# Gate vectors as weighted row sums inside the feed-forward networks, one condition's sums on ScalarE and GpSimd, and a shared tile for two score maps

## The chip, the core and the metric

The kernel runs on one core of a Trainium2 chip. The metric is the device time of one execution in microseconds (us), as the median of several runs. One execution is also recorded by the hardware profiler: its span goes from its first to its last instruction, and all times in the trace count from the start of that span.

Five engines work side by side, each with its own queue, in which instructions run in order: TensorE (PE, with its weight loads shown apart as PEld), VectorE (DVE), ScalarE (ACT), GpSimd (POOL) and SyncE (SP), which here only issues transfers (SPq).

## The reference

Two layers of a trunk act on three blocks of 128 tokens: block 0 is context under one condition vector, blocks 1 and 2 are latent tokens under another. In each layer a vector of six parts (shift, scale and gate, twice) is made from each condition by one large product, and modulates a mixer and a SwiGLU network:

```python
for l in range(DEPTH):
    mod = jax.nn.silu(cond) @ w_mod[l] + b_mod[l]
    sh1, sc1, g1, sh2, sc2, g2 = jnp.split(mod[:, None, :], 6, axis=-1)
    u = layer_norm(x) * (1.0 + sc1) + sh1
    ...   # layer 0: h = mixer_ab(u ...), layer 1: h = mixer_cd(u ...)
    x = layer_norm(ALPHA * x + g1 * h, ln_g[l, 0], ln_b[l, 0])
    u = layer_norm(x) * (1.0 + sc2) + sh2
    x = layer_norm(ALPHA * x + g2 * swiglu(u, w_gate[l], w_up[l], w_down[l]), ln_g[l, 1], ln_b[l, 1])
```

The model is 1024 wide, so each part needs a 1024x1024 slice of w_mod (4 MB) for two vectors. The part with index 5 is the gate g2, which is needed only when the network of its layer ends. Layer 1's mixer holds differential attention: for each of six heads two score maps of 64-wide queries and keys, softmax on each, and p0 - lam * p1:

```python
s = jnp.einsum('bqhmd,bkhmd->bhmqk', qb, keys).astype(f32) * (HEAD_DIM ** -0.5)
p = jax.nn.softmax(s, axis=-1)
p = p[:, :, 0] - lam_full * p[:, :, 1]
```

## The kernel before

**Order of the work.** Layer 0's mixer (to about 204 us), its output projection with the two normalisations (`w_out_phase`, to about 271 us), its network (`ffn_phase`, to about 541 us), then the same for layer 1: mixer with the scores (to about 674 us), output projection (to about 747 us), network (to the end). The program is written in order, and a scheduler that runs before the kernel does gives each engine its fixed sequence: of the instructions that it expects to be ready, the earliest in the program goes first, and those in `boost` (so also `hmm`) go ahead of others. Semaphores and buffer reuse are set by it too. `gated()` places an instruction behind one that is named.

**Weights.** Each weight unit of 128x1024 comes by a transfer on SP's queue into one of five `raw` buffers, ScalarE casts it (L173) to a part `r`, VectorE subtracts (L175) to get a rest `l`, and TensorE multiplies with both; five pairs `wr`/`wl` hold them. A network runs in half steps: 48 products for `wg` or `wu`, then, as long as there are any, 18 for `dn` with one unit of w_down.

**Two ways to make a part of the modulation.** (1) `mod_pe`: eight raw units of w_mod (`rawm`), each multiplied on TensorE with the two condition columns as weights, 32 products of 256 columns on four column groups. `mod_now` uses it in the output stage for (0, 5) and (1, 5), where `WMODS` names them; its products have the tile name `mw` and line L229. In `WORDER` this is the letter M, between the network's head for block 1 (H1) and that for block 2 (H2). (2) `mod_steps`: eight steps, one for each unit (`mraw`, L243). For each condition c a tile `z[c]` gathers the unit's rows, weighted by a column of `cs`: ScalarE writes the first (L246), VectorE adds the other seven (L249). Then eight products with a column of ones (L254) sum over the partitions, and VectorE adds the bias. `SMODS` names the five parts of layer 1 that are made so during layer 0's network, at most four steps to a call and a pause after each part; calls come twice for each of ten pairs of chunks, and a part is summed up in the third call after the one before. Tiles `z`, `mraw` and those of the residuals (`so`, `sd`) share four buffers (`big`, tag `s`).

A gate (v of 2 or 5) is then written by eight small transfers (L285) on SP's queue to memory and read back as a broadcast (`load_g`, L417).

**Head of the network.** `head(b)` makes the first 256 columns of the gate and up products (`hg`, `hu`) for one block, as soon as `to_u(b)` has made that block's input `u2` (its last instruction is `ulf` on L333).

**Scores in layer 1.** `sc1(b, h)` makes both maps of one block and head, `sc2` the softmax's rest. Each map has a bank of its own out of four, a product on half of the rows (64 of 128), a maximum on VectorE (L1217) and an exponential on ScalarE (L1223). Layer 0's windowed attention (`win1`) already takes two maps in a tile of two banks (`ws`, with one maximum over both, L872).

Of the kernel before, what the change touches and what calls it, by code (L numbers as in the profile page):

```python
# [14 lines left out]
AF = mybir.ActivationFunctionType  # L15
ALU = mybir.AluOpType
AX = mybir.AxisListType
PSUM = bass.MemoryType.PSUM

P = 128  # L20
# [5 lines left out]
NFP = D_FF // 256  # L26
HOLD = 4
RHOLD = (3, 5)
WMODS = (((0, 5),), ((1, 5),))
TMODS = ()  # L30
SMODS = (((1, 1), (1, 0), (1, 3), (1, 4), (1, 2)), ())
NLNW = 8
AORDER = "Q0 R0 W4 T G0 D V0 M0 Q1 W12 M1 G1 C0 E M2 N1 R1 N2 V1 C1 X N0 N4 N3 N5"
NIDLE = (5, 4)
# [30 lines left out]
def trunk_kernel(ctx: ExitStack, tc: tile.TileContext, a: dict):  # L65
    nc = tc.nc
    mm = nc.tensor.matmul
    V, S, G, SY = nc.vector, nc.scalar, nc.gpsimd, nc.sync
# [4 lines left out]
    def opened(name, **kw):  # L73
        st = ExitStack()
        return st.enter_context(pool(name, **kw)), st
# [6 lines left out]
    def bankA(name):  # L82
        return psA.tile([P, 512], F32, tag="A", name=name)
# [19 lines left out]
    def small(shape, name):  # L103
        tick[0] += 1
        n = 1
        for s in shape[1:]:
            n *= s
        return perm.tile(shape, F32, tag=f"sm{n}", name=f"{name}{tick[0]}", bufs=SMALL[n])

    def big(shape, name):  # L110
        return perm.tile(shape, F32, tag="s", name=name, bufs=4)

    def mid(shape, name):
        return perm.tile(shape, F32, tag="uf", name=name, bufs=3)

    def boost(f, *args, **kw):
        with tc.high_priority(offset=BOOST):
            return f(*args, **kw)  # L118

    def hmm(*args, **kw):  # L120
        return boost(mm, *args, **kw)
# [24 lines left out]
    cs = const.tile([P, 2, KC], F32, name="cs")  # L146
# [22 lines left out]
    def gated():  # L169
        return tc.issue_after(gate[0].ins) if gate[0] is not None else nullcontext()  # L170
# [43 lines left out]
    def mod_tile(l, v):  # L214

        bm = perm.tile([P, 256], F32, tag="bm", name=f"bm{l}_{v}", bufs=2)
        if v in (2, 5):
            bsrc = a["b_mod"][l, v * D : (v + 1) * D].rearrange("(j n) -> j n", j=4)
            for j in range(4):
                S.dma_start(bm[32 * j : 32 * j + 32, :], bsrc[j : j + 1, :].broadcast_to([32, 256]))  # L220
        return bm
# [15 lines left out]
    def mod_steps(l, v, out):  # L237
        w = a["w_mod"][l].rearrange("(p k) n -> p k n", k=KC)
        bm = mod_tile(l, v)
        z = [big([P, D], f"z{l}_{v}_{c}") for c in range(2)]  # L240
        for k in range(KC):
            t = big([P, D], f"mraw{l}_{v}_{k}")
            SY.dma_start(t, w[:, k, v * D : (v + 1) * D])  # L243
            for c in range(2):
                if k == 0:
                    S.mul(z[c], t, cs[:, c, k : k + 1])  # L246
                else:
                    with gated():
                        V.scalar_tensor_tensor(z[c], t, cs[:, c, k : k + 1], z[c], ALU.mult, ALU.add)  # L249
            yield k == KC - 1  # L250
        ps = bankA(f"mod{l}_{v}")
        for c in range(2):
            for j in range(4):
                mm(ps[32 * j : 32 * j + 32, c * 256 : (c + 1) * 256], ones, z[c][:, j * 256 : (j + 1) * 256],  # L254
                   start=True, stop=True)

        if v in (2, 5):
            V.scalar_tensor_tensor(bm, ps[:, 0:256], selc[:, 0:1], bm, ALU.mult, ALU.add)
        else:
            V.tensor_scalar(bm, ps[:, 0:256], selc[:, 0:1], None, ALU.mult)  # L260
        V.scalar_tensor_tensor(bm, ps[:, 256:512], selc[:, 1:2], bm, ALU.mult, ALU.add)
        out.append((bm, ps))
# [887 lines left out]
    def mixer_cd(u, cat, pto, u1, t1):  # L1150
        o_k = a["o_diff_k"][0, 0].rearrange("t h m d -> t (h m d)")
        o_v = a["o_diff_v"][0, 0].rearrange("t h d -> t (h d)")
        slab = cd_slab
        bk = Banks("pcd", S=4)
        ap, ap_es = opened("attn_cd")
        rope_of[0] = ap.tile([P, 2, 2, 64], F32, name="rope1")
        S.dma_start(rope_of[0], a["k_rope"].rearrange("b p s d -> p b s d"))
        if True:
            nlam, sub = lamd["nlam"], lamd["sub"]
            dqT = ap.tile([P, H_DIFF, NTOK], F32, name="dqT")  # L1160
            dkT = ap.tile([P, H_DIFF, 512], F32, name="dkT")
# [4 lines left out]
            for i, n in ((0, 4), (4, 2)):  # L1166
                t = mid([P, 512], f"ck{i}")
# [38 lines left out]
            def sc1(b, h):  # L1206
                nk = 1 if b == 0 else 3
                k0 = 0 if b == 0 else P
                w = nk * P
                nm = small([P, 2], "dnm")  # L1210
                sums = small([P, 2], "dsum")
                pss = []
                for m in range(2):
                    rows = slice(64 * m, 64 * m + 64)
                    ps = bk("S", f"ds{b}_{h}_{m}")
                    hmm(ps[:, 0:w], dqT[rows, h, b * P : (b + 1) * P], dkT[rows, h, k0 : k0 + w], start=True, stop=True)
                    V.reduce_max(nm[:, m : m + 1], ps[:, 0:w], AX.X)  # L1217
                    pss.append(ps)
                V.tensor_scalar(nm, nm, -0.125, None, ALU.mult)
                pm = []  # L1220
                for m in range(2):
                    t = ap.tile([P, 384], F32, tag="p", name=f"dp{b}_{h}_{m}", bufs=5)
                    S.activation(t[:, 0:w], pss[m][:, 0:w], AF.Exp, bias=nm[:, m : m + 1], scale=0.125,  # L1223
                                 accum_out=sums[:, m : m + 1])
                    pm.append(t)
                st_of[b, h] = (pm, sums)
# [18 lines left out]
            def scores(upto):  # L1245
                while state["n2"] < upto:
                    while state["n1"] < min(state["n2"] + 2, len(items)) and (state["n1"] < upto or upto == len(items)):
                        sc1(*items[state["n1"]])
                        state["n1"] += 1
                    sc2(*items[state["n2"]])  # L1250
                    state["n2"] += 1
# [59 lines left out]
            for b in range(NB):  # L1311
                ps = bankA(f"cd4_{b}")
# [6 lines left out]
            for b in range(NB):  # L1319
                ps = bankA(f"cd3_{b}")  # L1320
# [23 lines left out]
    m = {}  # L1344
    xscr = dram.tile([NB, P, D], F32, tag="xscr", name="xscr")
    for l in range(2):
# [9 lines left out]
        if l == 0:  # L1356
            def mod_ab(v, bk):
                mp = mod_pe(0, v, bk("M", f"mod0_{v}"))
                if v == 2:
                    m[0, v] = mod_scratch(mp, f"0_{v}")  # L1360
                else:
                    m[0, v] = mod_cols(mp, 0, v, bk("M", f"modt0_{v}"))

            pre, wxr_es = mixer_ab(u, cat, early, early_es, ap1, ap1_es, pto, *first, [lambda bk, v=v: mod_ab(v, bk) for v in (2, 3, 4)])
        else:
            cat, cat_es = open_cat(1)
            mixer_cd(u, cat, pto, m["s1"], m["t1"])
            pre, wxr_es = [], None
# [11 lines left out]
        hh = tuple(lnp.tile([P, NHEAD, NTOK], F32R, name=f"hh{q}{l}") for q in "rl")  # L1380
        w_out_phase(l, pre, cat, x, gt, lnv, u2, m[l, 3], m[l, 4], wx, hh, bankTO, WMODS[l])
        if wxr_es is not None:
# [37 lines left out]
        def all_mods(todo):  # L1420
            for ll, v in todo:
                out = []
                for pause in mod_steps(ll, v, out):
                    yield pause
                nm = f"{ll}_{v}"
                if v in (2, 5):
                    m[ll, v] = mod_scratch(out[0][0], nm)
                else:
                    m[ll, v] = mod_cols(out[0][0], ll, v, out[0][1])

        gen = all_mods(SMODS[l])

# [90 lines left out]
```

## Time and profile before

| | us |
|---|---|
| three runs: median (lowest to highest) | 1020.04 (1017.32 to 1021.83) |
| profiled execution: its own time | 1018.55 |
| profiled execution: span | 1016.8 |
| TensorE busy | 996.9 |
| VectorE busy | 637.9 |
| ScalarE busy | 432.9 |
| GpSimd busy | 1.2 |

The span is 1.75 us shorter than the time of the same execution; that difference lies outside of the instructions. The profiled execution lies 1.49 us under the median of the three runs. Busy time of TensorE is modelled at the ends of its instructions, so a stretch that is all busy can still hold short gaps. The granted clock was 0.997 of full over the span.

### The profile page before, as it was taken

Reading aid. Unit: us, or ns where it says so; the run is one execution under the profiler, and the core shown is the slowest. Engines: PE = TensorE matmul, PEld = TensorE weight load, DVE = VectorE, ACT = ScalarE, POOL = GpSimd, SP = SyncE. Lnnn points to the kernel's source line nnn. Section 1 sums busy time; section 2 is a strip of 40 time slices with the busy share of each in tenths; the row PEclk is TensorE's granted clock in tenths of the full one; section 3 lists DMA queues with packets and bytes.
Section 4 is the critical chain, followed back from the end, with each engine's and each line's share of the span. In section 5 each row is a group of like instructions: output and inputs, shape, how many; then the busy total and the mean of one; then the engine's idle time right before and its main releaser. Section 6 shows DMA issues by size and latency. Waiting matters only on the chain.

```text
span 1016.8 us, 14891 instructions
## 1 busy us (share of the span) xinstructions
PE 996.9 (98%) x5679; PEld 829.7 (82%) x5679; DVE 637.9 (63%) x1356; ACT 432.9 (43%) x786; POOL 1.2 (0%) x5
## 2 busy tenths in 40 slices
PE   9999999999999999999999999999999999999996
PEld 4775567688898988989987766787889999999985
DVE  5477558588785977968567677558843333335554
ACT  3385533227543333333428555544833333333410
POOL 0000000000000000000000000000000000000000
PEclk9999999999999999999999999999999999999998
DMA  9975446472896767676615322235574444444401
GB/s 305 294 203 187 146 132 205 171 254 94 281 301 219 217 211 253 208 235 208 207 63 161 95 88 93 83 103 224 184 252 146 125 125 124 125 125 127 161 22 41
DMA packets 109703, 172.85 MB, mean 170 GB/s; under 512 B 10176, under 2 KB 78272, under 8 KB 109632
## 3 DMA queue, kind: packets, MB, share of 16 engines
q1 hardware_dynamic: 106960, 170.87, 52.8%
q10 hardware_dynamic: 2672, 1.04, 0.4%
q8 instruction: 44, 0.72, 0.3%
q14 instruction: 27, 0.22, 0.1%
HBM read 167.52 MB, written 4.36 MB: 169 GB/s over the span
## 4 chain that ended last, share of the span: by engine, by line
PE 91%; DMA 3%; DVE 3%; ACT 2%; issue 1%; ACTq 0%; DVEq 0%
PE dn L518 17%; PE wu L542 17%; PE wg L542 17%; PE cd L377 8%; PE wo L377 6%; PE rvg L377 3%; PE s L377 3%; PE rqk L377 2%; DMA rawm<-in_w_mod 2%; PE ds L118 2%; PE hg L377 2%; PE mod L118 1%; PE hu L377 1%; PE ms L118 1%; PE po L118 1%; PE wpo L118 1%
## 5 line engine op out<-in xcount | busy, mean ns | idle before, releaser
L542 PE MATMUL wg<-ulf,r_wg 128*128 128x384 f32 x320 | 108.4, 339 | 0.0
L542 PE MATMUL wu<-ulf,r_wu 128*128 128x384 f32 x320 | 108.3, 338 | 0.0
L542 PE MATMUL wu<-urf,r_wu 128*128 128x384 f32 x320 | 108.2, 339 | 0.0
L542 PE MATMUL wg<-urf,l_wg 128*128 128x384 f32 x320 | 108.1, 338 | 0.0
L542 PE MATMUL wu<-urf,l_wu 128*128 128x384 f32 x320 | 108.1, 338 | 0.0
L542 PE MATMUL wg<-urf,r_wg 128*128 128x384 f32 x320 | 108.0, 339 | 0.0
L175 DVE TENSOR_TENSOR l_wg<-raw_wg,r_wg 128x1024 fp32r<-128x1024 f32 x40 | 48.7, 1223 | 68.4 <-ACT r_wg L173 68.4
L249 DVE SCALAR_TENSOR_TENSOR z<-mraw,cs,z 128x1024 f32<-128x1024 f32 x70 | 86.3, 1280 | 8.3 <-DMA mraw<-in_w_mod 8.0
L175 DVE TENSOR_TENSOR l_wd<-raw_wd,r_wd 128x1024 fp32r<-128x1024 f32 x36 | 44.0, 1223 | 53.7 <-ACT r_wd L173 53.7
L173 ACT CAST r_wd<-raw_wd 128x1024 fp32r<-128x1024 f32 x36 | 37.8, 1050 | 87.0 <-PE wu L542 40.1
L175 DVE TENSOR_TENSOR l_wu<-raw_wu,r_wu 128x1024 fp32r<-128x1024 f32 x40 | 48.6, 1222 | 40.1 <-ACT r_wu L173 40.1
L173 ACT CAST r_wg<-raw_wg 128x1024 fp32r<-128x1024 f32 x40 | 42.0, 1050 | 73.0 <-PE dn L518 29.9
L173 ACT CAST r_wu<-raw_wu 128x1024 fp32r<-128x1024 f32 x40 | 42.0, 1049 | 64.6 <-issue 24.2
L518 PE MATMUL dn<-l_wd,hr 128*128 128x512 f32 x168 | 66.6, 396 | 0.0
L518 PE MATMUL dn<-r_wd,hr 128*128 128x512 f32 x168 | 66.5, 396 | 0.0
L518 PE MATMUL dn<-r_wd,hl 128*128 128x512 f32 x168 | 66.5, 396 | 0.0
L542 PEld LDWEIGHTS wg<-urf,r_wg 128*128 128x128 f32 x320 | 60.1, 188 | 1.9 <-issue 0.8
L542 PEld LDWEIGHTS wu<-urf,r_wu 128*128 128x128 f32 x320 | 60.1, 188 | 1.7 <-ACT r_wg L173 0.8
L542 PEld LDWEIGHTS wu<-ulf,r_wu 128*128 128x128 f32 x320 | 60.1, 188 | 0.5
L542 PEld LDWEIGHTS wg<-ulf,r_wg 128*128 128x128 f32 x320 | 60.1, 188 | 0.5
L542 PEld LDWEIGHTS wg<-urf,l_wg 128*128 128x128 f32 x320 | 60.1, 188 | 0.0
L542 PEld LDWEIGHTS wu<-urf,l_wu 128*128 128x128 f32 x320 | 60.1, 188 | 0.0
(418 smaller groups left out, 2180.0 us busy)
## 6 DMA issues: line engine op xcount, KB each, us to landing
raw_wd<-in_w_down SPq DMA_DIRECT2D x44, 512.0 KB
rawm<-in_w_mod SPq DMA_DIRECT2D x40, 512.0 KB
mraw<-in_w_mod SPq DMA_DIRECT2D x40, 512.0 KB
raw_wg<-in_w_gate SPq DMA_DIRECT2D x40, 512.0 KB
raw_wu<-in_w_up SPq DMA_DIRECT2D x40, 512.0 KB
raw_cd<-in_w_in_cd SPq DMA_DIRECT2D x20, 512.0 KB
ms<-in_w_mod SPq DMA_DIRECT2D x16, 512.0 KB
raw_rqk<-in_w_in_ab SPq DMA_DIRECT2D x16, 256.0 KB
```

Source lines behind the costliest of these rows:

```text
L118: return f(*args, **kw)
L173: S.copy(r, t)
L175: V.tensor_tensor(lo, t, r, ALU.subtract)
L249: V.scalar_tensor_tensor(z[c], t, cs[:, c, k : k + 1], z[c], ALU.mult, ALU.add)
L377: op = mm(ps[:, col : col + width], u[pu][:, k0 + kk, b * P : (b + 1) * P], (r, lo)[pw][:, kk, :], start=(first and i == 0 and pu + pw == ...
L518: mm(acc[b, nh], h[fc][ph][:, b * P : (b + 1) * P], wrl[pw][:, nh * 512 : (nh + 1) * 512], start=(fc == 0 and ph + pw == 0), stop=(last an ...
L542: mm(ps[j][:, 0:NTOK], un[i][pw][:, k, j * P : (j + 1) * P], u2[pu][:, 4 * i + k, :], start=(i == 0 and k == 0 and pu + pw == 0), stop=(i ...
```

## The change

Three things change. The parts (0, 5) and (1, 5) leave the output stages (`WMODS`) and go to `SMODS`: (0, 5) is now the first of six parts made during layer 0's network, (1, 5) the only one during layer 1's. In `mod_steps` the second condition's seven later rows are no longer added on VectorE: ScalarE multiplies the unit in place by the condition's column, and GpSimd adds it to `z[1]`. In the scores the two maps of a block and head take one tile of two banks, of which there are two, both products are issued one behind the other, and one maximum runs over both.

```diff
-WMODS = (((0, 5),), ((1, 5),))
+WMODS = ((), ())
-SMODS = (((1, 1), (1, 0), (1, 3), (1, 4), (1, 2)), ())
+SMODS = (((0, 5), (1, 1), (1, 0), (1, 3), (1, 4), (1, 2)), ((1, 5),))
...
                     with gated():
-                        V.scalar_tensor_tensor(z[c], t, cs[:, c, k : k + 1], z[c], ALU.mult, ALU.add)
+                        if c == 0:
+                            V.scalar_tensor_tensor(z[c], t, cs[:, c, k : k + 1], z[c], ALU.mult, ALU.add)
+                        else:
+                            S.mul(t, t, cs[:, c, k : k + 1])
+                            G.tensor_tensor(z[c], z[c], t, ALU.add)
...
-        bk = Banks("pcd", S=4)
+        bk = Banks("pcd", S=2)
...
-                pss = []
+                ps = bk.pair("S", f"ds{b}_{h}")
                 for m in range(2):
                     rows = slice(64 * m, 64 * m + 64)
-                    ps = bk("S", f"ds{b}_{h}_{m}")
-                    hmm(ps[:, 0:w], dqT[rows, h, b * P : (b + 1) * P], dkT[rows, h, k0 : k0 + w], start=True, stop=True)
-                    V.reduce_max(nm[:, m : m + 1], ps[:, 0:w], AX.X)
-                    pss.append(ps)
+                    hmm(ps[:, m, 0:w], dqT[rows, h, b * P : (b + 1) * P], dkT[rows, h, k0 : k0 + w], start=True, stop=True)
+                V.reduce_max(nm, ps[:, :, 0:w], AX.X)
...
-                    S.activation(t[:, 0:w], pss[m][:, 0:w], AF.Exp, bias=nm[:, m : m + 1], scale=0.125,
+                    S.activation(t[:, 0:w], ps[:, m, 0:w], AF.Exp, bias=nm[:, m : m + 1], scale=0.125,
                                  accum_out=sums[:, m : m + 1])
```

## Rows read from the trace of the kernel before

**Rows 1.** the page: busy time, share of the span and instructions of each engine

```profile
PE 996.9 (98%) x5679; PEld 829.7 (82%) x5679; DVE 637.9 (63%) x1356; ACT 432.9 (43%) x786; POOL 1.2 (0%) x5
```

**Rows 2.** busy time by stretch (us, instructions), granted clock, DMA share and GB/s

```profile
245.40:265.10 19.70, 19.70 (x182) 15.68 (x181) 14.42 (x43) 17.32 (x33) 0.00 (x0) 1.00 0.64 217
272.00:512.00 240.00, 240.00 (x1326) 222.91 (x1325) 181.07 (x188) 89.76 (x109) 0.00 (x0) 1.00 0.72 229
545.00:645.00 100.00, 98.00 (x455) 68.23 (x453) 69.44 (x177) 60.59 (x153) 0.00 (x0) 1.00 0.29 91
719.80:739.00 19.20, 19.20 (x182) 15.57 (x181) 13.88 (x43) 13.56 (x29) 0.00 (x0) 1.00 0.58 182
```

**Rows 3.** the same table for the instructions of tile mw alone

```profile
245.40:265.10 19.70, 5.50 (x64) 1.93 (x64) 0.00 (x0) 1.00 0.64 217
719.80:739.00 19.20, 4.88 (x64) 1.79 (x64) 0.00 (x0) 1.00 0.58 182
```

**Rows 4.** timeline of layer 0, output stage (start us, us, what)

```profile
261.49 0.69 DVE L333 TENSOR_TENSOR ulf<-ufo,urf 128x512 fp32r<-128x512 f32 x1
...
265.04 0.39 PE L377 MATMUL hg<-r_gh,urf 128*128 128x256 f32 x1
```

**Rows 5.** timeline of layer 1, output stage

```profile
736.33 0.69 DVE L333 TENSOR_TENSOR ulf<-ufo,urf 128x512 fp32r<-128x512 f32 x1
...
738.95 0.39 PE L377 MATMUL hg<-r_gh,urf 128*128 128x256 f32 x1
...
746.84 0.44 PE L118 MATMUL ht<-ident,hsg 128*128 128x128 f32 x2 [1.22 <-DVE hsg L480]
```

**Rows 6.** SP's queue, layer 1, output stage

```profile
693.20 32.61 SPq L164 DMA_DIRECT2D rawm<-in_w_mod  x6
```

**Rows 7.** the chain that ended last, layer 0's network (start us, us, what)

```profile
321.90 1.00 PE mod L254 x16
...
361.56 1.00 PE mod L254 x16
...
476.29 1.00 PE mod L254 x16
...
502.82 8.45 PE wu L542 x48
511.27 9.71 PE dn L518 x42
```

**Rows 8.** groups of instructions, shapes apart (busy us, mean ns, idle before)

```profile
L249 DVE SCALAR_TENSOR_TENSOR z<-mraw,cs,z 128x1024 f32<-128x1024 f32 x70 | 86.3, 1280 | 8.3 <-DMA mraw<-in_w_mod 8.0
...
L175 DVE TENSOR_TENSOR l_wg<-raw_wg,r_wg 128x1024 fp32r<-128x1024 f32 x40 | 48.7, 1223 | 68.4 <-ACT r_wg L173 68.4
...
L566 DVE TENSOR_TENSOR hl<-sg,hr 128x384 fp32r<-128x384 f32 x36 | 19.8, 554 | 7.5 <-ACT hr L565 7.5
...
L246 ACT ACTIVATE z<-mraw,cs 128x1024 f32<-128x1024 f32 x10 | 11.5, 1154 | 10.3 <-DVE z L249 10.3
```

**Rows 9.** the same view for GpSimd

```profile
L847 POOL MEMSET s<- 128x1024 f32 x1 | 1.0, 952 | 0.3 <-POOLq L1509 0.3
```

**Rows 10.** SP's queue, then VectorE: one gate group of layer 0's network

```profile
329.13 2.72 SPq L243 DMA_DIRECT2D mraw<-in_w_mod  x2
...
332.85 4.98 DVE L249 SCALAR_TENSOR_TENSOR z<-mraw,cs,z 128x1024 f32<-128x1024 f32 x4 [0.21 <-DMA mraw<-in_w_mod]
```

**Rows 11.** TensorE among the scores of layer 1

```profile
596.40 0.91 PE L118 MATMUL ds<-dkT,dqT 64*128 64x384 f32 x2
```

**Rows 12.** groups by shape again: products of the scores

```profile
L118 PE MATMUL ds<-dkT,dqT 64*128 64x384 f32 x48 | 14.9, 530 | 0.2
...
L118 PE MATMUL ws<-wkT,wqT 64*128 64x384 f32 x32 | 8.2, 535 | 0.0
...
L118 PE MATMUL ds<-dkT,dqT 64*128 64x128 f32 x24 | 4.9, 322 | 0.7 <-ACT dp L1223 0.7
```

**Rows 13.** who waited for whom, weight loads, 545 to 645 us (total, times, longest)

```profile
PEld ds L118 <- ACT dp L1223: 3.3, 6, 1.1
```

## The prediction

> **What bounds the kernel now.** I read the page's busy times first: TensorE is busy for 98% of the span [rows 1], so the question is never which engine is fullest, but in which stretch TensorE could have less to do, and in which it would start to wait. The table of stretches is to be read for the engine that is *not* at its limit: in layer 0's network TensorE is busy for 240.0 of 240 us, VectorE for 181.1, ScalarE for 89.8 [rows 2]. Relief of VectorE is worth nothing there by itself; VectorE, ScalarE and GpSimd only matter by being late. The same table for tile mw alone, and the timelines around the head of block 2, say what the moved gates cost in the output stages [rows 3 to 5]. The chain of waits gives the rhythm of the gate sums in the network [rows 7], the groups the price of each step [rows 8, 9], the two queues the turn-round of a unit's buffer [rows 10].
>
> **Output stages, what is removed.** The 64 records of mw take 5.50 us of TensorE in layer 0 and 4.88 us in layer 1 [rows 3]. This work also filled a gap, since block 2's input is late there. In layer 0 the stretch from the last product of the projection to block 2's head lasts 19.7 us, all busy [rows 2]; without mw, 14.2 us of work are left, done at about 259.6. The head of block 2 needs the first half of ulf, done at 261.49 + 0.69 = 262.18, and started at 265.04 [rows 4]. So 2.9 us come off, not 5.5. In layer 1, 19.2 - 4.88 = 14.3 us of work end at 734.1, the half is there at 736.33 + 0.69 = 737.02, the head started at 738.95 [rows 5]: 1.9 us come off. A wait of 1.22 us follows in layer 1, for hsg on VectorE [rows 5]. VectorE was behind there with rests of weight units that had come late, for six rawm transfers occupy SP's queue for 32.6 us ahead of them, waiting for raw buffers [rows 6]. With them the lateness should go: 1.2 us. Sum: 6.0 us off. Bounds: nothing, if the chain to ulf takes up all of the time, and 5.5 + 4.9 + 1.2 = 11.6 us, if it moves forward by as much as TensorE does.
>
> **What comes back in the networks.** Each gate now takes sixteen records with the ones column, 1.00 us of the chain [rows 7]. Both networks are full on TensorE, so nothing hides it: 2.0 us on. The transfers move, 16 units of 512 KB as before; eight small gate writes and four bias loads go with each gate. They stand in the queues of the network instead of ahead of its first weights, with raw buffers of their own no longer in the way. The adds of layer 1's gate meet a slack VectorE: I cost them at nothing, as there is one group of some 40 us in a network that lasts from 747 us to the end, and the gate is read only near that end.
>
> **The rhythm in layer 0.** A group has 39.66 us from product to product (321.90 to 361.56) [rows 7]. Before, a buffer turns round in a transfer (issue at 329.13, first add at 332.85: 3.7 us [rows 10]) and two adds of 1.28 us [rows 8], 6.3 us; with two buffers that is 3.1 us a step and 25 us a group, hidden by 14 us. After, it is 3.7 us, one add of 1.28, a multiplication on ScalarE of 1.15 (like L246) [rows 8], and GpSimd's add. No row shows that add. Its nearest row is GpSimd's own memset of the same shape, 0.952 us [rows 9], which moves one stream. From below I bound it by that, from above by three streams one after another, 2.86 us. I take two, 1.9 us, since the two inputs must be read and the write can follow behind. Then a turn is 8.0 us, a step 4.0 us, and a group 8 x 4.0 + 3.7 = 35.7 us, inside 39.66. At 2.86 us it is 39.7 us, just at the edge. ScalarE takes 42 such multiplications and two first rows more, 51 us on 89.8 of 240 [rows 2, 8]: room enough. In its queue each waits for VectorE's add, and the casts of weight units stand behind; their cover is the five pairs of weight buffers, behind which VectorE now idles for 68 us of the whole kernel ahead of l_wg alone, waiting for casts [rows 8]. If that cover went, every us of delay would be one of TensorE.
>
> The sixth group is tighter. With the down products used up, the third call after 476.29 falls at 502.82, after 26.5 us [rows 7], and the group wants 35.7: 9.2 us late (13.2 at the upper bound). TensorE has 8.45 + 9.71 us of other work from there on [rows 7], and its sequence is set by expected readiness; mw's own records stood scattered through other products. I cost it at nothing, with 18.2 us of cover.
>
> **Scores.** VectorE saves one start in two of its maxima, beside a full TensorE (98.0 of 100 us) [rows 2]: nothing. TensorE itself may save: where the two maps of a head stand apart, one takes 0.91 us alone [rows 11], while layer 0's pairs, in a shared tile, take 8.2 / 8 = 1.03 us for both [rows 12]. Twelve large items at 1.03 are 12.3 us against 14.9. A small map takes 4.9 / 12 = 0.41 us; six small pairs at 1.03 / 0.91 of that, 0.46, are 2.8 us against 4.9 [rows 12]: 4.7 us off in all. If each pair ran like one map, 12 x 0.91 + 6 x 0.41 = 13.4 us stand against 19.8, and 6.4 come off. Against it, both banks are now free only after the second exponential. The weight loads waited 3.3 us for exponentials [rows 13]; if that doubles, it costs 3.3 us. I take 3.0 us off, between -6.4 and +3.3.
>
> **Sum.** -6.0 + 2.0 - 3.0 = -7.0 us. Against the profiled execution's 1018.55 us that is 1011.6; it lay 1.49 us under the median of the runs, so for a median I say **1013 us**. All best bounds give -11.6 + 2.0 - 6.4 = -16.0 (1004), all worst ones of this course +5.3 (1025).
>
> **Rivals.** *The two engines exclude each other (slower).* If VectorE's instructions with two inputs in SBUF cannot run while GpSimd adds, a group's time is a sum over both: nine weight rests at 1.22, three hl at 0.55, seven adds at 1.28 [rows 8], 21.6 us, plus 7 adds of GpSimd. At 1.9 us that is 34.9 of 39.66, at 2.86 us 41.6; from 2.58 us on it decides. At 2.86 four groups are late by 1.9 us each, and the last by 41.6 - 26.5 = 15.1: 23 us, so 1036 us. For it: VectorE is already busy for 75% there [rows 2], nearly all on such instructions. Against it: no row before has GpSimd at work beside VectorE at all. The Trainium skill speaks for it ("SBUF — State Buffer", section "Who interferes with whom"): a VectorE instruction with two SBUF inputs and a GpSimd one that reads SBUF share a port, and the second to start waits until the first ends; no run here shows it yet. Its page "GPSIMD Engine Reference", section 3.1, times a GpSimd add of 2048 columns at 4497 ns; an estimate from that is 2.25 us for 1024, with which a step would be 4.2 us and the sum the same. Chance 0.17.
>
> *The last group is waited for.* Its product stays at the third call and TensorE waits 9.2 us: 1022 us. For it: the text puts it there. Against: the scattered mw. Chance 0.15.
>
> *The gates were free filler.* The chain to ulf keeps its pace, nothing comes off in the output stages, and the pairs give no more than their waits take: +2.0, 1022 us. For it: ScalarE is busy for 17.3 of the 19.7 us there [rows 2]. Against: the half of ulf is there 2.9 us early. Chance 0.13.
>
> *Everything removed comes off*: 11.6 instead of 6.0, 1007 us. Chance 0.05. Mine: 0.50, with a range of its own of 1008 to 1018.
>
> **Numbers.** Faster or slower by over 0.5% (5.1 us), which is about what a measurement of this kernel can tell from no change, means under 1014.9 or over 1025.1. Faster: 0.84 of mine and the full return, 0.47. Slower: the exclusion and its neighbours, 0.22. Within: 0.31. The range of 1006 to 1028 leaves out the exclusion at its price and the extreme of the full return.
>
> **What would show it.** Right: no mw, head of block 2 under 3 us after its ulf; in layer 0's network no wait of TensorE for z, GpSimd's adds under 2.3 us, and VectorE's adds still at 1.28; four records of ds together each time. Wrong: L249 or L175 with longer means than before (exclusion), TensorE waiting for z at each group or at the last, casts of weights waiting for VectorE's adds, ds waiting longer for dp.

## The result, and the profile after

The changed kernel takes 1060.55 us (median of four runs, 1058.83 to 1064.77) against 1019.37 us before (four runs beside it): ratio 1.041, 95% interval 1.0378 to 1.0442. It is slower by 41 us, where 7 us less were forecast. The profiled execution has a span of 1063.0 us at a granted clock of 0.98.

The page's line of busy times, which answers to [rows 1]:

```profile
PE 1004.1 (94%) x5583; PEld 837.4 (79%) x5583; DVE 672.4 (63%) x1319; ACT 486.0 (46%) x839; POOL 131.4 (12%) x54
```

TensorE has fallen from 98% to 94%: it waits now. VectorE has 37 instructions less and 34.5 us *more* of busy time, so its instructions must have become longer. The groups by shape, which answer to [rows 8] (busy us, mean ns of one, idle time before), show which:

```profile
L253 POOL TENSOR_TENSOR z<-z,mraw 128x1024 f32<-128x1024 f32 x49 | 130.2, 2657 | 687.2 <-ACT mraw L252 671.6 <-PE wg L546 14.9
...
L250 DVE SCALAR_TENSOR_TENSOR z<-mraw,cs,z 128x1024 f32<-128x1024 f32 x49 | 82.1, 1676 | 40.5 <-DMA mraw<-in_w_mod 40.4
...
L175 DVE TENSOR_TENSOR l_wu<-raw_wu,r_wu 128x1024 fp32r<-128x1024 f32 x40 | 62.5, 1564 | 36.3 <-ACT r_wu L173 36.3
...
L252 ACT ACTIVATE mraw<-mraw,cs 128x1024 f32<-128x1024 f32 x49 | 56.2, 1151 | 103.3 <-DVE z L250 100.4 <-issue 2.6 <-ACT r_wd L173 0.3
...
L175 DVE TENSOR_TENSOR l_wg<-raw_wg,r_wg 128x1024 fp32r<-128x1024 f32 x40 | 52.5, 1312 | 54.6 <-ACT r_wg L173 54.3
...
L570 DVE TENSOR_TENSOR hl<-sg,hr 128x384 fp32r<-128x384 f32 x36 | 34.3, 952 | 7.1 <-ACT hr L569 6.9
...
L563 DVE TENSOR_TENSOR sg<-wu,sg 128x384 f32<-128x384 f32 x40 | 22.1, 553 | 4.1 <-PE wu L546 4.1
```

The sums went from 1280 to 1676 ns, the rests from 1223 to 1564 (l_wu) and 1312 (l_wg), hl from 554 to 952 [rows 8]. Only sg kept its 553 ns: it has the shape of hl, but one of its inputs (wu) comes from PSUM. ScalarE's multiplication, new here, takes 1151 ns, as estimated from L246. VectorE's timeline over some 10 us of layer 0's network, and GpSimd's (start us, us, what), show how one instruction gets long:

```profile
375.34 3.25 DVE L250 SCALAR_TENSOR_TENSOR z<-mraw,cs,z 128x1024 f32<-128x1024 f32 x1 [1.54 <-DMA mraw<-in_w_mod]
378.51 0.55 DVE L563 TENSOR_TENSOR sg<-wu,sg 128x384 f32<-128x384 f32 x1
...
380.26 2.61 DVE L570 TENSOR_TENSOR hl<-sg,hr 128x384 fp32r<-128x384 f32 x1
```

```profile
375.11 2.39 POOL L253 TENSOR_TENSOR z<-z,mraw 128x1024 f32<-128x1024 f32 x1 [10.73 <-ACT mraw L252]
379.97 2.49 POOL L253 TENSOR_TENSOR z<-z,mraw 128x1024 f32<-128x1024 f32 x1 [2.46 <-ACT mraw L252]
```

GpSimd's add begins at 375.11 and ends at 377.50. VectorE's sum begins 0.23 us behind it and ends at 378.59, 1.09 us after GpSimd: it had stood nearly all of the add. The hl at 380.26 does the same behind the second add.

Over the whole trace, 37 of VectorE's sums, rests and hl began while an add ran. The 14 sums and 16 rests among them ended 1.08 to 1.12 us behind the add and the seven hl 0.41 to 0.42, however early in the add they had begun; the sums that overlapped with no add took 1269 to 1286 ns. So they waited for the add's end, and did not run beside it at a lower speed.

Where the time went is read from the first product of each stage in the timelines (us; "gates and tile" and "tile only" are two experiments below):

| stage, from first to first product | before | after | gates and tile, sums on VectorE | tile only |
|---|---|---|---|---|
| layer 0: block 0's head (hg) to network (wg) | 25.4 | 24.7 | 23.3 | 25.4 |
| layer 0's network to layer 1 (cd) | 270.6 | 316.3 | 273.7 | 270.7 |
| layer 1's mixer and projection to head (hg) | 178.3 | 173.0 | 173.0 | 173.1 |
| layer 1: head to network (wg) | 25.0 | 23.8 | 23.8 | 25.0 |
| layer 1's network to the end of the span | 272.0 | 279.8 | 272.3 | 271.2 |

The loss is in the two networks: 45.7 and 7.8 us against before. The other stages gained a little, the scores' one 5.3 us. Two stretches, layer 0's network (272 to 512, beside [rows 2]) and 12.4 us of layer 1's, in the table of stretches (us, then PE, PEld, DVE, ACT, POOL busy, granted clock, DMA share, GB/s):

```profile
272.00:512.00 240.00, 216.83 (x1135) 195.08 (x1134) 160.87 (x132) 109.25 (x125) 93.00 (x35) 0.97 0.63 198
...
813.60:826.00 12.40, 12.28 (x53) 12.13 (x54) 8.25 (x7) 6.48 (x9) 2.81 (x1) 0.76 0.57 165
```

TensorE is busy for 216.8 of 240 us in place of all, although VectorE, in which it all begins, is busy for only 160.9: VectorE is not full, it is late. Whom it makes late is read in the timeline around one of TensorE's waits, here over three engines, and behind it in the chain of waits (start us, us, what):

```profile
393.51 1.28 DVE L250 SCALAR_TENSOR_TENSOR z<-mraw,cs,z 128x1024 f32<-128x1024 f32 x1 [2.54 <-DMA mraw<-in_w_mod]
...
394.88 1.15 ACT L252 ACTIVATE mraw<-mraw,cs 128x1024 f32<-128x1024 f32 x1 [5.03 <-DVE z L250]
395.93 0.47 ACT L556 ACTIVATE sg<-wg 128x384 f32<-128x384 f32 x1
...
396.46 0.69 PE L546 MATMUL wu<-urf,r_wu 128*128 128x384 f32 x1 [2.23 <-ACT sg L556]
```

```profile
387.05 2.84 POOL z L253
...
389.91 3.51 DMA mraw<-in_w_mod
...
393.51 1.30 DVE z L250
```

The product at 396.46 wants nothing from the gate sums. It waits for sg, which in ScalarE's queue stood behind the multiplication, which waited 5.03 us for VectorE's sum, which had waited for its unit. That unit's transfer could be issued (389.91) only when GpSimd's add of an earlier one (387.05) had set its buffer free. So a late sum holds up work of the network itself.

### The profile page after: what moved, and what is told of

Its sections match the earlier page's. It is cut to its first block, busy times and chain, and to the rows that moved or that the text cites. A ratio compares the mean times of both kernels' runs of the same rounds, so it can differ in the third digit from the quotient of the medians.

```text
span 1063.0 us, 14880 instructions
## 1 busy us (share of the span) xinstructions
PE 1004.1 (94%) x5583; PEld 837.4 (79%) x5583; DVE 672.4 (63%) x1319; ACT 486.0 (46%) x839; POOL 131.4 (12%) x54
## 4 chain that ended last, share of the span: by engine, by line
PE 60%; DVE 14%; DMA 10%; ACT 7%; POOL 4%; issue 4%; SPq 0%; ACTq 0%; DVEq 0%; POOLq 0%
PE dn L522 11%; PE wg L546 10%; PE wu L546 9%; PE cd L381 7%; DMA mraw<-in_w_mod 5%; POOL z L253 4%; PE wo L381 4%; DVE z L250 3%; PE rvg L381 3%; PE s L381 2%; DMA rawm<-in_w_mod 2%; ACT mraw L252 2%; PE rqk L381 2%; PE mod L118 1%; PE ms L118 1%
## 5 line engine op out<-in xcount | busy, mean ns | idle before, releaser
L253 POOL TENSOR_TENSOR z<-z,mraw 128x1024 f32<-128x1024 f32 x49 | 130.2, 2657 | 687.2 <-ACT mraw L252 671.6
L546 PE MATMUL wg<-urf,r_wg 128*128 128x384 f32 x320 | 113.6, 356 | 14.4 <-DVE sg L563 14.3
L546 PE MATMUL wg<-ulf,r_wg 128*128 128x384 f32 x320 | 112.4, 351 | 0.0
L546 PE MATMUL wg<-urf,l_wg 128*128 128x384 f32 x320 | 112.0, 350 | 0.0
L250 DVE SCALAR_TENSOR_TENSOR z<-mraw,cs,z 128x1024 f32<-128x1024 f32 x49 | 82.1, 1676 | 40.5 <-DMA mraw<-in_w_mod 40.4
L252 ACT ACTIVATE mraw<-mraw,cs 128x1024 f32<-128x1024 f32 x49 | 56.2, 1151 | 103.3 <-DVE z L250 100.4
L175 DVE TENSOR_TENSOR l_wd<-raw_wd,r_wd 128x1024 fp32r<-128x1024 f32 x36 | 52.1, 1446 | 59.2 <-ACT r_wd L173 59.2
L175 DVE TENSOR_TENSOR l_wg<-raw_wg,r_wg 128x1024 fp32r<-128x1024 f32 x40 | 52.5, 1312 | 54.6 <-ACT r_wg L173 54.3
L175 DVE TENSOR_TENSOR l_wu<-raw_wu,r_wu 128x1024 fp32r<-128x1024 f32 x40 | 62.5, 1564 | 36.3 <-ACT r_wu L173 36.3
L522 PE MATMUL dn<-l_wd,hr 128*128 128x512 f32 x168 | 66.6, 396 | 0.0
L546 PEld LDWEIGHTS wg<-ulf,r_wg 128*128 128x128 f32 x320 | 63.5, 198 | 0.3
```

Of the source, the lines that this page charges most:

```text
L175: V.tensor_tensor(lo, t, r, ALU.subtract)
L252: S.mul(t, t, cs[:, c, k : k + 1])
L253: G.tensor_tensor(z[c], z[c], t, ALU.add)
L522: mm(acc[b, nh], h[fc][ph][:, b * P : (b + 1) * P], wrl[pw][:, nh * 512 : (nh + 1) * 512], start=(fc == 0 and ph + pw == 0), stop=(last an ...
L546: mm(ps[j][:, 0:NTOK], un[i][pw][:, k, j * P : (j + 1) * P], u2[pu][:, 4 * i + k, :], start=(i == 0 and k == 0 and pu + pw == 0), stop=(i ...
```

## Experiments

Two theories were set against each other. **Theory 1, turn-round:** a unit's buffer is held through transfer, VectorE, ScalarE and GpSimd, and the queues of three engines stand behind that chain. **Theory 2, exclusion:** VectorE's instructions with two inputs in SBUF and GpSimd's adds can't run at the same time. A third, that a sixth group is too much for layer 0's network, was tried first. All medians are of four or more runs.

**Undoing the second condition's chain.** `e1_no_chain` is the changed kernel with

```
-                        if c == 0:
-                            V.scalar_tensor_tensor(z[c], t, cs[:, c, k : k + 1], z[c], ALU.mult, ALU.add)
-                        else:
-                            S.mul(t, t, cs[:, c, k : k + 1])
-                            G.tensor_tensor(z[c], z[c], t, ALU.add)
+                        V.scalar_tensor_tensor(z[c], t, cs[:, c, k : k + 1], z[c], ALU.mult, ALU.add)
```

> The changed kernel with the second condition's adds back on VectorE; the gates stay in the networks and the two maps in one tile. Theory 1 (the turn of a buffer: transfer, VectorE's add, ScalarE's multiplication, GpSimd's add, with the queues of three engines standing behind it) and theory 2 (VectorE and GpSimd exclude each other) both expect the whole 45 us of layer 0's network to go: 1009 to 1018 us, sums on VectorE at a mean of 1.28 us again. Theory 3 (a sixth group with its transfers and small writes is too much for layer 0's network) expects 1050 to 1062 us.

Measured: 1012.0 us, ratio to before 0.9941 (0.9926 to 0.9956). Everything comes back, the sums take 1281 ns again, and the sixth group costs little beside them: theory 3 falls.

**Only the chain.** `e2_chain_only` is the kernel before with that edit reversed: five parts, gates in the output stages, maps apart.

> The kernel before with nothing but the second condition's adds moved to ScalarE and GpSimd: five parts, gates in the output stages, maps apart. Theories 1 and 2: five groups in place of six, so about 5/6 of 45 us less what a group that ends in the network's free part loses: 1045 to 1058 us. Theory 3: within 5 us of before, 1015 to 1025 us.

Measured: 1049.41 us, 1.0308 (1.0288 to 1.0328). Five groups cost 31 us. Its groups show the same mark as after, hl longer and sg not:

```profile
L570 DVE TENSOR_TENSOR hl<-sg,hr 128x384 fp32r<-128x384 f32 x36 | 28.3, 785 | 7.5 <-ACT hr L569 7.5
...
L563 DVE TENSOR_TENSOR sg<-wu,sg 128x384 f32<-128x384 f32 x40 | 22.2, 554 | 5.4 <-PE wu L546 5.4
```

**Only the shared tile.** `e3_tile_only` is the kernel before with `Banks("pcd", S=2)`, `bk.pair` and one maximum over both maps.

> The kernel before with nothing but the shared tile for the two score maps. All theories leave it alone; the recorded term is 3.0 us off, so 1014 to 1018 us, the products of the scores at 10.7 us for the large maps as in the changed kernel. If a shared tile is waited for, 1020 to 1024 us.

Measured: 1012.29 us, 0.9947 (0.9931 to 0.9964): 5.9 us off by the medians, more than the 3.0 forecast and just under the range expected. The groups of the large and the small maps, for [rows 12]:

```profile
L118 PE MATMUL ds<-dkT,dqT 64*128 64x384 f32 x48 | 10.7, 530 | 0.0
...
L118 PE MATMUL ds<-dkT,dqT 64*128 64x128 f32 x24 | 3.0, 323 | 0.4 <-ACT dp L1221 0.4
```

**The add on VectorE, behind the multiplication.** `e5_add_on_vector` changes one letter of the changed kernel, so that the chain stays and GpSimd is idle:

```
-                            G.tensor_tensor(z[c], z[c], t, ALU.add)
+                            V.tensor_tensor(z[c], z[c], t, ALU.add)
```

> The changed kernel with only GpSimd's add moved to VectorE: ScalarE still multiplies in place, then VectorE adds, so GpSimd is idle and VectorE has two instructions for a unit again. Theory 2 (exclusion) expects 1010 to 1020 us, as with the adds back on VectorE. Theory 1 (turn-round with queues that stand) expects a large part of the loss to stay, as VectorE still has to wait for ScalarE in the middle of a unit: the turn is 3.7 + 1.28 + 1.15 + 1.28 = 7.4 us in place of some 8.5 to 9, so 1025 to 1050 us.

Measured: 1016.36 us, 0.9981 (0.9966 to 0.9997). The chain is there (ScalarE still waits 62.5 us for z), but it costs 4.4 us over `e1_no_chain`, not 48. Theory 1 as stated missed its range.

**A longer turn without GpSimd.** `e7_longer_turn` adds a second pass to that:

```
                             S.mul(t, t, cs[:, c, k : k + 1])
+                            S.mul(t, t, 1.0)
                             V.tensor_tensor(z[c], z[c], t, ALU.add)
```

> The changed kernel with the add on VectorE, and ScalarE going over the unit a second time (times 1.0), so that the turn is 3.7 + 1.28 + 2 x 1.15 + 1.22 = 8.5 us against 9.2 as measured in the changed kernel (with 1.68 and 2.66), again with GpSimd idle. Theory 1: the loss comes back, 1035 to 1060 us. Theory 2: near the kernel with one multiplication, 1014 to 1024 us.

Measured: 1031.41 us, 1.0131 (1.0108 to 1.0155), outside both ranges: 15 us for 1.06 us more of turn (8.4 in place of 7.4), and of ScalarE's time for each unit. The table below, behind the runs with more buffers, shows where: at the last group, and not in the pace of the others.

**A shorter turn with GpSimd.** `e6_no_multiplication` deletes `S.mul` from the changed kernel: the kernel leaves out the second condition's weights and adds its later rows as they are.

> The changed kernel without ScalarE's multiplication: GpSimd adds the second condition's later rows unweighted, as soon as they have landed. The turn is 3.7 + 1.28 + 2.4 = 7.4 us, as short as with the add on VectorE behind the multiplication (7.4, 1016 us), and ScalarE waits for nobody. Theory 1: 1012 to 1022 us. Theory 2, with GpSimd's 49 adds all there: most of the loss stays, 1040 to 1060 us.

Measured: 1063.36 us, 1.0446 (1.0423 to 1.047): no relief at all, and above both ranges. Both engines now start on a unit as it lands, and meet more often; in the groups the add and the sum both grow, so the turn was not short either (3.7 + 2.27 + 2.93 = 8.9 us):

```profile
L252 POOL TENSOR_TENSOR z<-z,mraw 128x1024 f32<-128x1024 f32 x49 | 143.5, 2928 | 664.5 <-DMA mraw<-in_w_mod 662.9 <-POOL z L252 0.3
...
L250 DVE SCALAR_TENSOR_TENSOR z<-mraw,cs,z 128x1024 f32<-128x1024 f32 x49 | 111.3, 2271 | 15.4 <-DMA mraw<-in_w_mod 15.1
```

**More buffers.** `e10_four_buffers` is the changed kernel, `e11_four_buffers_on_vector` is `e1_no_chain`, both with

```
-HOLD = 4
+HOLD = 2
...
-            t = big([P, D], f"mraw{l}_{v}_{k}")
+            t = mrp[0].tile([P, D], F32, tag="mraw", name=f"mraw{l}_{v}_{k}", bufs=4)
...
```

> The changed kernel with four buffers for the units of w_mod in place of two (two of the four held-back units of w_down give up their room). A turn of 9.2 us is then 2.3 us a step, so it sets no pace. Theory 1: the loss goes, 1012 to 1030 us. Theory 2: most of it stays, 1040 to 1062 us, with VectorE's sums still over 1.6 us.

> The control for the run with four buffers: the same buffers, but the second condition's adds on VectorE. 1008 to 1016 us by all theories; what it lies off 1012 us is the price of the buffers themselves.

Measured: 1056.87 us (1.0384, 1.0351 to 1.0417) and 1016.61 us (0.9986, 0.9969 to 1.0002). The control lies 0.6 us above its range: the buffers, with the two held-back units that they replace, cost 4.6 us. The chain costs 40.3 us over its control, against 48.5 with two buffers, though sums now hardly wait for units (3.5 us in place of 40.4):

```profile
L254 POOL TENSOR_TENSOR z<-z,mraw 128x1024 f32<-128x1024 f32 x49 | 147.8, 3016 | 655.4 <-ACT mraw L253 653.2
...
L251 DVE SCALAR_TENSOR_TENSOR z<-mraw,cs,z 128x1024 f32<-128x1024 f32 x49 | 100.4, 2049 | 4.0 <-DMA mraw<-in_w_mod 3.5
```

So some 8 of 48 us went with the scarce buffers, and 40 stayed.

**Where the groups lose it.** The table is read from the timelines of layer 0's network. It gives the time from the first product of one group's sum (tile mod, with z and the column of ones) to that of the next; the first time counts from the first wg, the last runs to layer 1 (cd).

| us | 1st group | 2nd | 3rd | 4th | 5th | 6th | to layer 1 |
|---|---|---|---|---|---|---|---|
| `e1_no_chain` | 51.0 | 39.5 | 39.7 | 39.6 | 35.4 | 31.1 | 37.4 |
| `e5_add_on_vector` | 51.0 | 39.2 | 39.7 | 39.7 | 37.1 | 37.4 | 32.7 |
| `e7_longer_turn` | 50.9 | 39.2 | 40.0 | 40.7 | 38.2 | 45.8 | 35.6 |
| after | 52.9 | 40.5 | 48.6 | 47.1 | 46.9 | 43.6 | 36.7 |
| `e10_four_buffers` | 66.6 | 41.0 | 44.0 | 46.9 | 44.0 | 31.2 | 32.9 |
| `e11_four_buffers_on_vector` | 51.0 | 39.2 | 39.6 | 39.6 | 39.6 | 31.2 | 32.9 |

With a turn of 8.4 us and GpSimd idle, the first five groups keep their pace within about a us, and 11.3 of the 13.7 us by which `e7_longer_turn` is over `e5_add_on_vector` here come at the sixth group and behind it. With GpSimd's adds the changed kernel gets late from the third group on, by 7.5 to 12.5 us a group over `e1_no_chain`. Four buffers bring the sixth group back to its control's 31.2 us and leave the first five late by 33.5 us in sum.

**Quarter adds.** `e8_quarter_adds` cuts GpSimd's add in the changed kernel:

```
-                            G.tensor_tensor(z[c], z[c], t, ALU.add)
+                            for j in range(4):
+                                q = slice(256 * j, 256 * j + 256)
+                                G.tensor_tensor(z[c][:, q], z[c][:, q], t[:, q], ALU.add)
```

> The changed kernel with GpSimd's add cut into four instructions of 256 columns. If it is the sum of both engines' times that counts, nothing is won: 1055 to 1068 us. If it is the length of one GpSimd instruction, behind which VectorE stands with all that is queued, VectorE gets in between: means of sums and rests near 1.4 us and 1025 to 1045 us. Theory 1 (turn-round, 4 x 0.61 = 2.45 us for an add): 1055 to 1065 us.

Measured: 1082.8 us, 1.0637 (1.0599 to 1.0676), worse than all three expected. VectorE did get in between, its sums falling to 1390 ns, but the four adds of a unit now take 4 x 1007 ns in place of 2657 (the shortest quarter took 716, and four of these are 2.9 us), the turn gets longer, and VectorE waits 97.2 us for units:

```profile
L255 POOL TENSOR_TENSOR z<-z,mraw 128x256 f32<-128x256 f32 x196 | 190.6, 1007 | 648.2 <-ACT mraw L252 648.2
...
L250 DVE SCALAR_TENSOR_TENSOR z<-mraw,cs,z 128x1024 f32<-128x1024 f32 x49 | 68.1, 1390 | 97.3 <-DMA mraw<-in_w_mod 97.2
```

**Adds beside the sums, that nobody waits for.** These leave the kernel before as it is, all sums on VectorE, and let GpSimd add on a tile of its own at each later step of layer 0's gate sums. `e4_side_adds` and `e4h_half_side_adds` start them by a memset of VectorE into one of two cells (four adds a step, or two):

```
...
                         V.scalar_tensor_tensor(z[c], t, cs[:, c, k : k + 1], z[c], ALU.mult, ALU.add)
+                        if c == 0:
+                            V.memset(pin[k % 2], 0.0)
+                            for _ in range(4):
+                                G.tensor_tensor(side[0], side[0], pin[k % 2].broadcast_to([P, 256]), ALU.add)
...
```

> The kernel before, and beside each of the 35 later steps of the gate sums in layer 0's network GpSimd makes four adds of 128x256 on a tile of its own that nobody waits for; VectorE keeps all sums. No turn of a buffer gets longer. Theory 2 (exclusion): VectorE's instructions with two inputs in SBUF get longer (sums over 1.40 us, rests over 1.30), and as they and GpSimd together want about 170 + 35 x 4 x 0.65 = 261 of layer 0's 240 us, the time grows by 10 to 40 us, 1030 to 1060 us. Theory 1 (turn-round): no change, 1015 to 1021 us.

> The same with two side adds a step in place of four. Theory 2: 170 + 45 = 215 of 240 us, so VectorE still has room; its means grow by about half as much, and the time by 0 to 15 us, 1017 to 1033 us. Theory 1: no change, 1015 to 1021 us.

Measured: 1073.96 us (1.0552, 1.0535 to 1.0569) and 1042.39 us (1.024, 1.0223 to 1.0258). Both lie above both ranges, but they don't decide: the memset of a cell had to wait until GpSimd had read it (50.2 and 25.8 us in all), so VectorE's queue stood behind GpSimd by a semaphore. `e4b_side_adds_unwaited` was to mend that, with seven cells and four adds of 224 columns.

> The kernel before with side adds on GpSimd again, four of 128x224 a step (about 0.54 us each, worked out from 612 ns for 256 columns, so 35 x 4 x 0.54 = 76 us), now with a pin for each of a group's seven steps, so that VectorE no longer waits for GpSimd by a semaphore anywhere. Theory 2 (exclusion): VectorE's instructions with two inputs in SBUF still get longer, and the time grows by 5 to 30 us, 1023 to 1048 us. Theory 1 (turn-round): no change, 1015 to 1021 us, and the first side-add run was slow through its own waits alone.

Measured: 1060.91 us (1.0422, 1.0388 to 1.0457), above both ranges, and its own premise fell: the memsets, which depend on nothing, ran ahead by a group and waited again. From its waits (who for whom: us in total, times, longest):

```profile
DVE pin L253 <- POOL side L255: 33.8, 17, 2.5
```

The next set ties each start to the sum before it, with 35 cells that are never used again, and one held-back unit less for room:

```
...
+                        if c == 0:
+                            pin = sidep[0].tile([P, 1], F32, name=f"pin{l}_{v}_{k}")
+                            V.tensor_scalar(pin, z[0][:, 0:1], 0.0, None, ALU.mult)
+                            G.tensor_tensor(side[0], side[0], pin.broadcast_to([P, D]), ALU.add)
...
```

`e13_side_add_1024` is this, `e14_pins_only` leaves out the last line, `e15_side_add_512` adds 512 columns, `e16_side_memsets` has a 128x1 add and two memsets of 128x1024 there (they write a tile and read none).

> The kernel before with three held-back units in place of four (for room), and at each of the 35 later steps of layer 0's gate sums one GpSimd add of 128x1024 on a tile of its own, started by a 128x1 instruction of VectorE behind the first condition's sum, with a cell of its own for each step. No engine waits for GpSimd, and every engine's order of instructions is that of the control. Theory 2 (exclusion): VectorE's sums, rests and hl get longer by about one collision of up to 2.4 us a step, and with 170 + 35 x 2.4 = 254 of 240 us TensorE falls behind: 20 to 55 us over the control. Theory 1 (turn-round and waits of the chain): within 4 us of the control.

> The control: the same kernel with the 35 small instructions of VectorE, but without GpSimd's adds. All theories: 1014 to 1024 us.

> The same side adds on 512 columns, about 1.2 us each, half of the dose: 170 + 35 x 1.2 = 212 of 240 us. Theory 2: longer VectorE instructions, by half as much in sum, and a loss well under half of that with 1024 columns, 2 to 20 us over the control. Theory 1: within 4 us of the control.

> In place of each side add two GpSimd memsets of 128x1024 (952 ns each before, 1.9 us a step), which write and read nothing. If every GpSimd instruction keeps VectorE out, the loss is near that of the adds, 15 to 45 us over the control, and VectorE's means rise; if only one that reads operands does, as the Trainium skill has it (SBUF — State Buffer, Who interferes with whom), within 4 us of the control and VectorE's means as before.

| | us | ratio to before (95%) | over pins only | VectorE busy, us | its sums, mean ns |
|---|---|---|---|---|---|
| pins only | 1018.55 | 1.0011 (0.9993 to 1.0029) | | 638.3 | 1280 |
| add of 1024 columns | 1056.63 | 1.0382 (1.034 to 1.0424) | 38.1 | 692.5 | 1887 |
| add of 512 columns | 1031.53 | 1.0115 (1.0078 to 1.0152) | 13.0 | 662.6 | 1558 |
| two memsets | 1018.2 | 1.0002 (0.9984 to 1.002) | -0.4 | 638.5 | 1281 |

No wait for GpSimd is in any of these traces, and VectorE, ScalarE and TensorE run the same instructions in the same order with the adds of 1024 columns, with the memsets and with the pins only. The groups with the 1024 columns, and then with the memsets:

```profile
L251 DVE SCALAR_TENSOR_TENSOR z<-mraw,cs,z 128x1024 f32<-128x1024 f32 x70 | 129.3, 1887 | 10.6 <-DMA mraw<-in_w_mod 10.6
...
L255 POOL TENSOR_TENSOR side<-side,pin 128x1024 f32<-128x1024 f32 x35 | 88.9, 2539 | 171.7 <-DVE pin L254 171.7
...
L569 DVE TENSOR_TENSOR sg<-wu,sg 128x384 f32<-128x384 f32 x40 | 22.1, 553 | 5.4 <-PE wu L552 5.4
```

```profile
L251 DVE SCALAR_TENSOR_TENSOR z<-mraw,cs,z 128x1024 f32<-128x1024 f32 x70 | 86.9, 1281 | 6.4 <-DMA mraw<-in_w_mod 6.3
...
L255 POOL TENSOR_TENSOR side<-side,pin 128x1 f32<-128x1 f32 x35 | 40.5, 1157 | 116.4 <-DVE pin L254 115.9
...
L256 POOL MEMSET side<- 128x1024 f32 x35 | 33.4, 956 | 2.1
```

Adds that no engine waits for make VectorE 54.2 us longer and the kernel 38.1 us slower; half the columns, 24.3 and 13.0 us; GpSimd busy with memsets beside the same sums, nothing. Theory 2 is shown, and with it which instructions exclude each other: of GpSimd those that read, and of VectorE those with two inputs in SBUF, as sg keeps its 553 ns. Its size here is a guide to the changed kernel's, not the same number, as VectorE has all sums in these runs.

## Why the prediction was wrong

The step that failed is **the rhythm in layer 0**. It added up a turn from transfer, VectorE's add at 1.28, ScalarE and GpSimd's add at 1.9, found a step of 4.0 and a group of 35.7 inside 39.66 us, and let VectorE and GpSimd work side by side. On these instructions they can't: the sum took 1.68 and the add 2.66 us, rests and hl grew with them, and layer 0's network lasted 42.6 us longer than with the sums on VectorE (316.3 against 273.7). The prediction had this as its first rival at 0.17, with the rule of the Trainium skill ("SBUF — State Buffer", section "Who interferes with whom") beside it, and set it aside because no row before had GpSimd at work beside VectorE. By that rule a VectorE instruction with two SBUF inputs keeps out a GpSimd instruction that reads SBUF, and the other way round, but not one that only writes: the runs agree on each, with 1887 ns in place of 1280 for sums and 2539 in place of 1892 for adds that read, and with 1281 for sums beside memsets.

**The rival was priced too low as well.** It let the loss begin where a group's sum over both engines exceeds 39.66 us, at 2.58 us for an add. GpSimd's add took about 2.39 us when it met nobody (2.66 in the mean), above the 1.9 taken and the 2.25 worked out beside the rival, and inside the bounds. By the rival's own sum that is 21.6 + 7 x 2.39 = 38.3 of 39.66 us, "inside", and yet the loss was 42.6 us, up to 12.5 for a group. So it does not begin only where the sum exceeds the time. The side adds of 512 columns show the same: 212 of 240 us by their expectation, and 13.0 us lost. A likely reason, which no run tests by itself, is that the work doesn't come without gaps: in the changed kernel the sums wait 40.4 us for transfers, and what stands behind them in three queues in order waits too.

**The turn-round** is a part of the loss, and mainly at the last group: four buffers in place of two take 8 of 48 us off, and bring the sixth group from 43.6 back to 31.2 us. A longer turn without GpSimd costs 15 us from 7.4 to 8.4 us of turn, but the groups before the last keep their pace, as the prediction's sum for a turn of 8.0 us has it. With exclusion the turn grew to 3.7 + 1.68 + 1.15 + 2.66 = 9.2 us, 1.2 us more than forecast. By the same sum a group then wants 8 x 4.6 + 3.7 = 40.5 us, only 0.8 more than it has, where the third to fifth took 47 to 49. The remaining 40 us were not divided further by a run.

**ScalarE's queue** was costed at nothing, with the five pairs of weight buffers as cover for its casts. That cover held: in layer 0's network TensorE waited for no weight unit. What stood in the queues without a cover was sg: TensorE waited 6.8 us there for ScalarE's part of it, as at 396.46 above, and 18.2 us for VectorE's. The multiplication is not the cause by itself, as nothing came back without it (`e6_no_multiplication`), and it cost 4.4 us where GpSimd was idle (`e5_add_on_vector`).

**The sixth group** was also costed at nothing. With the sums on VectorE that was about right: of TensorE's waits in that network only 0.9 us in all remain. The second rival, a last group waited for, did not come by itself. Behind the chain the sixth group was late by 12.5 us (43.6 against 31.1), though in all of that network TensorE waited only 2.1 us for a z.

**Layer 1's gate** was costed at nothing because it is read late. Its chain cost 7.5 us (279.8 against 272.3 with its sums on VectorE). One group is enough to make VectorE late for the network's own work, as the chain of waits shows (start us, us, what; "issue" is time in which the engine waited for nothing that the profile shows):

```profile
810.48 1.28 DVE l_wd L175
811.76 1.27 issue
813.03 0.56 DVE sg L563
...
813.72 11.34 PE wg L546 x48
```

A GpSimd add ran from 809.65 to 812.02. The rest that began at 810.48 ended only behind it, after 2.63 us, sg stood behind the rest, and the products of wg behind sg, for 2.86 us.

**Output stages**, 6.0 forecast: 2.1 in layer 0 and 1.2 in layer 1 came off (`e1_no_chain` against the shared tile alone), 3.3 in all. TensorE now reaches the heads early and waits 2.5 us for ulf, 1.3 us for hsg, so the chain to ulf took up more than the forecast left it. **What comes back**, 2.0 forecast: 3.0 and 1.1, so 4.1 us; sixteen records are 1.0 of each, and a wait of 0.9 in layer 0 is named above; the rest isn't assigned. Moving the gates was thus worth -3.3 + 4.1 = +0.8 us, where -4.0 was forecast; the medians of the two runs, 1012.0 and 1012.29, agree on "nothing".

**Scores**, 3.0 forecast: 5.3 us in the stage. Large and small maps came to 10.7 + 3.0 = 13.7 us from 19.8, where 12.3 + 2.8 were forecast and 13.4 was the bound: a large pair costs what one map had (10.7 / 12 = 0.89 us, against 0.91), a small one 0.50 against 0.41. The waits of weight loads for exponentials, feared to double from 3.3 us [rows 13], fell to 1.6. Here the mechanism was right, and the term of 3.0 too small by 2.3.

## What to carry over

Before work goes to GpSimd, look at what VectorE runs beside it: reading instructions of GpSimd and VectorE instructions with two inputs in SBUF are one queue in time, however idle either engine looks in the profile's shares, and here 1.28 us of VectorE were exchanged for 2.39 us of that queue. Add both engines' times as one resource and ask for much room, since a late instruction also holds up what stands behind it in its own queue, as sg did here. Of the three changes only the shared tile is worth its edit (1012.29 us); with the gates in the networks as well, and their sums on VectorE, the time is the same (1012.0 us). Either is 0.5 to 0.6% faster than the kernel before, with an interval clear of no change.

## What the runs showed of the hardware

A GpSimd add of a single column, 128x1, took about 190 ns where it met nobody, and 1157 in the mean: most of that is waiting for a VectorE instruction of 1.2 to 1.3 us to end. GpSimd often comes in between two instructions that VectorE issues back to back, but not always: 5 of these 35 adds waited 3.31 to 4.63 us, through three or four rests in a row, and no run shows why. So cutting an add doesn't shorten the waits in proportion; how much of the quarters' loss is that, and how much their greater length of 2.9 us in place of 2.39, no run divides. And a wait of TensorE costs more than itself: after 2.86 us of waiting for sg in layer 1, 48 products of wg took 11.34 us where 8.45 is usual, at a granted clock of 0.76 over those 12.4 us, a mean between the levels of 1.2 and 2.4 GHz. Over the kernel, the same 5583 products are busy for 1004.1 us after and for 985.0 us in `e1_no_chain`, so by the page's busy times about 19 of the 52.5 us between their spans are slower products and not waits.
